# Five places instead of seven in a bidirectional scan, and two more column pairs by seven products

## The chip, the cores and the metric

The kernel runs on one core of a Trainium2 chip. The metric is the device time of one execution in microseconds. The engines are TensorE (PE, matrix products; PEld is its weight load), VectorE (DVE), ScalarE (ACT), GpSimd (POOL) and SyncE (SP, which issues most transfers). Each engine takes its instructions in order; they wait for each other by semaphores.

## The reference, cut to what matters

One encoder layer on 1024 positions of width 1024, in float32:

```
h    = rmsnorm(x)
proj = h @ w_in                       # 8192 columns: glu 1024, q, v, z_f, z_b, og, g_a, g_b 1024 each
a    = pointwise(silu(layernorm(conv31(glu))))
o    = scan(q, 1 - f_f, v, f_f) + flip(scan(flip(q), flip(1 - f_b), flip(v), flip(f_b)))   # 8 heads of 128
       # per head: S_t = diag(f_t) S_{t-1} + k_t v_t^T,  o_t = S_t^T q_t
b    = (rmsnorm per head of o * silu(og)) @ o_w
x    = x + (sigmoid(g_a) * a + sigmoid(g_b) * b) @ w_out
x    = x + (silu(conv3(h2 @ w_gate)) * (h2 @ w_up)) @ w_down,   h2 = rmsnorm(x)
out  = rmsnorm(x)
```

The change touches the projection `h @ w_in`, where and how its columns are computed, and the scan over the heads.

## The kernel before, in words

**Products.** A float32 product is made of three fast ones (`mm3`, L147 to L149): each operand is split into a high and a low part, the split being a copy on ScalarE and a subtraction on VectorE (L123). A *tile* is 128 columns of the projection (`std_job`): 8 steps in depth x 3 x 2 halves of 512 positions = 48 products. A *pair* (`pair_job`) takes two tiles of columns and computes them as a 2 x 2 block product with seven products in place of eight (Strassen and Winograd): 7 x 4 x 3 = 84 products, with sums of weights and of results besides. 56 column tiles are in the list `todo`; the first 2 x `NPAIRS` of them are done in pairs, the others are *filler tiles*.

**Pieces.** Jobs are generators. One `fill(1)` of a `Stream` emits one piece, six products, at that place of the program. PE's order is the order of emission; the other engines' orders are set by a scheduler.

**Stages around the change.** The convolution with 31 taps runs on VectorE (`conv_steps`, L953 and L956: 4 x 31 steps), and after each tap `s_pairs.fill(CONV_FILL)` emits pieces of pairs. Then comes the LayerNorm, with more pieces of pairs, and the pairs are drained. Then comes the scan of the eight heads in two halves of 512 positions each, 16 halves in all, with the filler tiles and the pointwise product's tiles (`dense`) between its steps.

**The scan.** Inside a half, the decays are not applied position by position. Positions are doubled up: at level h (1, 2, 4, ... 64), every block of h positions is scored against its neighbour block, with keys and queries scaled by the decay up to the border between them. Keys `kG` and queries `qF` hold both directions; at each level they are multiplied in place by the block's total decay (`tb`), and `tb` is formed for the next level (`double`, three VectorE steps at L1052). A level of h up to 16 is 16 small products of 32 x 32 (`level`, L1103), whose stationary side is a copy `A` of the keys that interleaves the two directions (`key_blocks`, a ScalarE copy, L1083); the queries are read from `qF` itself. The levels of 32 and 64 are products by block (`blocks`, L1167). The diagonal is 16 x 2 small products (L1138), the two directions adding up in the bank. The results of the small levels are picked out of the bank into `D` through masks (`copy_predicated` on VectorE, L1153, L1187, L1189). A wide product of zeros (`none`, L1182) first fills the bank that levels 32 and 64 write only in part. `scan_states` transposes the doubled keys (L1203, banks `tr`), copies them (`kT`) and forms the states `Sf` and `Sb`; `scan_outputs` forms a head's outputs (L1253), which are squared and scaled on ScalarE (L1258, L1272), transposed back (L1279, banks `tr`) and multiplied by the gate on VectorE (L1281). A head's outputs run beside the next head's scan (`pending`).

**Places.** `scan_base` (levels 1, 2, 4) of the next half and `scan_levels` and `scan_states` (levels 8 to 64, states) of the present half run in step. Each `yield` of the latter two is a *place*: `between` emits `FILL` pieces of filler, one step of the next half's base and one step of the pending outputs. Before, a half has 4 + 3 = 7 places. PSUM has eight banks: three for `mm`, two for `sc`, two for `tr` and one for `ob`.

Of the kernel before, what the change touches and what calls it, by code (L numbers as in the profile page):

```python
# [10 lines left out]
F32 = mybir.dt.float32  # L11
# [5 lines left out]
AX = mybir.AxisListType  # L17

P = 128
FILL = 1.3  # L20
CONV_FILL = 1.6
NPAIRS = 19
LN_FILL = 6
LN_LAST = 12
GLU_FIRST = 4
# [21 lines left out]
def tile_hybrid_encoder(  # L47
# [54 lines left out]
    def page(pool, tag, bufs, dt=F32):  # L102
        return pool.tile([P, H], dt, tag=tag, name=nm(tag), bufs=bufs)
# [941 lines left out]


    hp = tc.alloc_tile_pool(name="heads", bufs=1, reuse_waits="tile")
    none = hp.tile([P, H], mybir.dt.bfloat16, name="none")
    G.memset(none, 0.0)

    def tt(o, a, b, op=ALU.mult):
# [25 lines left out]
    def pairs(t, h, other=H):  # L1077

        return view(t, 0, [[other + h, 2], [2 * h, H // (2 * h)], [1, h]])

    def key_blocks(kG, h):
        A_t = page(hp, "A", 3)
        A.copy(pairs(A_t, h, 0), pairs(kG, h))  # L1083
        return A_t

    def slot(b, n):
        return b[:, n * P : (n + 1) * P]
# [7 lines left out]
    def each():  # L1095
        for c in range(4):
            for g in range(0, P, 32):
                yield c * P + g, slice(g, g + 32), slice(32 * c, 32 * c + 32)

    def level(b, A_t, qF, h):  # L1100

        for at, g, o in each():
            T.matmul(  # L1103
                b[g, o].rearrange("p (b x e) -> p b x e", x=2, e=h),
                A_t[:, at : at + 32],
                view(qF, at, [[2 * h, 16 // h], [H + h, 2], [1, h]]),
                start=True,
                stop=True,
            )

    def double(kG, qF, tb, h, to=None):

        n, nb = H // (2 * h), H // h
        tt(pairs(kG, h), pairs(kG, h), view(tb, 1, [[nb - 1, 2], [2, n], [0, h]]))
        tt(pairs(qF, h), pairs(qF, h), view(tb, nb + 1, [[-(nb + 1), 2], [2, n], [0, h]]))
        if to is None:
            tn = hp.tile([P, 2, n], F32, tag=f"tb{h}", name=nm("tb"), bufs=2)
            to = view(tn, 0, [[n, 2], [1, n]])
        else:
            tn = None  # L1120
        tt(to, view(tb, 0, [[nb, 2], [2, n]]), view(tb, 1, [[nb, 2], [2, n]]))
        return tn

    def scan_base(ins):


        q, f, kG, ks = ins
        qF = hp.tile([P, 2, H], F32, tag="qF", name=nm("qF"), bufs=4)
        D_t = hp.tile([P, 4, 32], F32, tag="D", name=nm("D"), bufs=3)
        for d in range(2):  # L1130
            V.tensor_scalar(kG[:, d, :], kG[:, d, :], ks[:, d : d + 1], None, op0=ALU.mult)
        A_t = key_blocks(kG, 1)
        tt(qF, view(q, 0, [[0, 2], [1, H]]), view(f, H, [[-H, 2], [1, H]]))
        yield
        b = bank("sc")
        for at, g, o in each():
            for d in range(2):
                T.matmul(  # L1138
                    slot(b, 3)[g, o],
                    kG[:, d, at : at + 32],  # L1140
                    q[:, at : at + 32],
                    start=d == 0,
                    stop=d == 1,
                )
        tb = f
        for n, h in enumerate((1, 2, 4)):
            level(slot(b, n), A_t, qF, h)
            tb = double(kG, qF, tb, h)
            A_t = key_blocks(kG, 2 * h)
            yield  # L1150
        A.copy(D_t, near(slot(b, 2)))
        for n, m in ((0, m_1), (1, m_2), (3, m_d)):
            V.copy_predicated(D_t, over(m), near(slot(b, n)))  # L1153
        yield qF, kG, A_t, tb, D_t

    def scan_levels(base, S_t, Tt):


        qF, kG, A_t, tb, D_t = base

        def blocks(b, h):

            for c in range(0, H, P):
                for s0 in range(0, P, h):
                    t0 = s0 ^ h
                    d = s0 // h % 2
                    T.matmul(  # L1167
                        b[s0 : s0 + h, c + t0 : c + t0 + h],
                        kG[:, d, c + s0 : c + s0 + h],
                        qF[:, 1 - d, c + t0 : c + t0 + h],  # L1170
                        start=True,
                        stop=True,
                    )

        for h in (8, 16, 32, 64):
            if h < 32:
                b = bank("ob")
                level(slot(b, 0), A_t, qF, h)
            else:
                if h == 32:  # L1180
                    b = bank("sc")
                    T.matmul(b, none[:, :P], none, start=True, stop=True)  # L1182
                blocks(b, h)
            tb = double(kG, qF, tb, h, view(Tt, 0, [[4, 2], [1, 4]]) if h == 64 else None)
            if h == 8:
                A_t = key_blocks(kG, 16)
                V.copy_predicated(D_t, over(m_8), near(slot(b, 0)))  # L1187
            elif h == 16:
                V.copy_predicated(D_t, over(m_16), near(slot(b, 0)))  # L1189
            elif h == 64:  # L1190
                A.copy(S_t, c4(b))
                for g in range(0, P, 32):
                    A.copy(S_t[g : g + 32, :, g : g + 32], D_t[g : g + 32])
            yield

    def scan_states(i, kG, v, Tt, Sf, Sb):

        half = i % 2
        kTs = []
        for d in range(2):  # L1200
            b = bank("tr")
            for c in range(4):
                T.transpose(b[:, c * P : (c + 1) * P], kG[:, d, c * P : (c + 1) * P], ident)  # L1203
            kT = page(hp, "kT", 2)
            A.copy(kT, b)
            kTs.append(kT)
            yield
        for d in range(2):
            u = bank("sc" if d else "ob")
            for c in range(4):  # L1210
                sl = slice(c * P, (c + 1) * P)
                T.matmul(u[:, sl], kTs[d][:, sl], v[:, c, :], start=True, stop=True)
            u4 = c4(u)
            if d == 0:
                for c in range(4 if half == 0 else 3):
                    nx = Sf[half][:, c + 1, :] if c < 3 else Sf[1][:, 0, :]
                    if half == 0 and c == 0:
                        V.tensor_copy(nx, u4[:, 0, :])
                    else:
                        V.scalar_tensor_tensor(  # L1220
                            nx,
                            Sf[half][:, c, :],
                            Tt[:, half, 0, c : c + 1],
                            u4[:, c, :],
                            op0=ALU.mult,
                            op1=ALU.add,
                        )
            else:

                A.copy(Sb[half][:, 0:3, :], u4[:, 1:4, :])  # L1230
                if half == 1:
                    A.copy(Sb[0][:, 3, :], u4[:, 0, :])
        yield
# [96 lines left out]
    for h in range(NH):  # L1330
        Tt = hp.tile([P, 2, 2, 4], F32, tag="Tt", name=nm("Tt"), bufs=3)
        Sf = [hp.tile([P, 4, DK], F32, tag="st", name=nm("Sf"), bufs=4) for _ in range(2)]
        Sb = [hp.tile([P, 4, DK], F32, tag="st", name=nm("Sb"), bufs=4) for _ in range(2)]
        kept = []
        for half in range(2):
            i = 2 * h + half
            base = cur.result()
            ahead = Base(ins) if i + 1 < NI else None
            ins = scan_inputs(i + 2) if i + 2 < NI else None

            def between(fill):
                dense.fill(fill)
                if ahead is not None:
                    ahead.step(BASE_STEPS)
                pending.fill(1)

            S_t = hp.tile([P, 4, P], F32, tag="S", name=nm("S"), bufs=3)
            vl = load(d_v[h][half])
            for n, _ in enumerate(scan_levels(base, S_t, Tt[:, half])):
                if n == 2:  # L1350
                    b = bank("tr")
                    for c in range(4):
                        T.transpose(b[:, c * P : (c + 1) * P], vl[:, c * P : (c + 1) * P], ident)
                    v = hp.tile([P, 4, DK], F32, tag="v", name=nm("v"), bufs=3)
                    A.copy(v.rearrange("p c e -> p (c e)"), b)
                between(FILL)
            qF, kG = base[:2]
            for _ in scan_states(i, kG, v, Tt, Sf, Sb):
                between(FILL)
            kept.append((S_t, v, qF))  # L1360
            cur = ahead
        pending = Stream(outputs(h, kept, Tt, Sf, Sb))
# [398 lines left out]
```

## Time and profile before

| | |
|---|---|
| median of three runs | 1810.12 us (1809.49 to 1810.22) |
| profiled execution | 1807.26 us, its span 1805.5 us |
| granted TensorE clock | 0.993 of full |
| PE busy over the span | 97% |
| VectorE, ScalarE busy | 67%, 45% |

The span is the time from the first to the last instruction of the profiled execution. Busy time of PE counts a product from its start to its modelled end, and neighbours overlap; the distance between the starts of two products is what one costs.

### The profile page before, as it was taken

How to read it: one execution, taken by the hardware profiler on the slowest of the kernel's cores; microseconds unless marked ns; L12 is line 12 of the kernel's file. 1: busy time of each engine (PE TensorE's matmuls, PEld its weight loads, DVE VectorE, ACT ScalarE, POOL GpSimd, SP SyncE). 2: the span in 40 equal slices, each digit the busy share in tenths (PEclk: the TensorE clock that was granted, in tenths of full speed). 3: DMA queues.
4: the chain of work that ended last, by engine and by line, in shares of the span. 5: the costliest groups of instructions: out<-in, count | busy, mean ns of one | idle time of the engine just before them, and what ended most of it. 6: DMA issues, size and time to landing. Idle time of an engine off the chain costs nothing.

```text
span 1805.5 us, 30702 instructions
## 1 busy us (share of the span) xinstructions
PE 1757.3 (97%) x12150; PEld 1433.9 (79%) x12150; DVE 1213.0 (67%) x1813; ACT 804.1 (45%) x1534; POOL 152.2 (8%) x165
## 2 busy tenths in 40 slices
PE   8989999999999999999989999999999999999997
PEld 6878877888877778877878888878888888888885
DVE  4599999657577777777545666766766766545355
ACT  6344332335466566756552245434434434422123
POOL 1201111000000000000000002011111111000000
PEclk9999999999999999999999999999999999999999
DMA  8658878746652333335358666576776765534233
GB/s 279 215 153 187 190 174 187 203 146 199 209 177 95 120 107 117 118 101 177 112 171 236 200 205 207 142 152 144 147 158 147 151 152 129 161 97 128 82 93 135
DMA packets 321270, 284.48 MB, mean 158 GB/s; under 512 B 14942, under 2 KB 242022, under 8 KB 321126
## 3 DMA queue, kind: packets, MB, share of 16 engines
q1 hardware_dynamic: 279958, 250.01, 44.0%
q0 software_dynamic: 41168, 32.51, 12.8%
q8 instruction: 95, 1.56, 0.3%
q14 instruction: 49, 0.40, 0.1%
HBM read 189.40 MB, written 76.81 MB: 147 GB/s over the span
## 4 chain that ended last, share of the span: by engine, by line
PE 72%; DVE 9%; DMA 7%; ACT 5%; issue 4%; POOL 1%; SPq 1%; POOLq 0%; ACTq 0%; DVEq 0%
PE mm L147 17%; PE mm L149 16%; PE mm L148 16%; PE sc L147 3%; PE sc L149 3%; PE sc L148 3%; DVE acc L956 2%; PE ob L1253 2%; DVE wp L123 2%; PE tr L147 2%; PE tr L149 2%; PE tr L148 2%; DMA ev<-d_ga 1%; PE sc L1103 1%; DMA wr<-in_w_in_dram 1%
## 5 line engine op out<-in xcount | busy, mean ns | idle before, releaser
L147 PE MATMUL mm<-hx,wp 128*128 128x512 f32 x1144 | 463.0, 405 | 9.3 <-DVE ev L718 4.9
L149 PE MATMUL mm<-hx,wp 128*128 128x512 f32 x1144 | 449.9, 393 | 2.1 <-DVE wp L123 2.0
L148 PE MATMUL mm<-hx,wp 128*128 128x512 f32 x1144 | 449.0, 392 | 0.0
L123 ACT CAST wp<-wr 128x1024 fp32r<-128x1024 f32 (+2 forms) x171 | 162.0, 948 | 342.9 <-PE mm L148 258.3
L147 PEld LDWEIGHTS mm<-hx,wp 128*128 128x128 f32 x1144 | 216.6, 189 | 56.1 <-DVE ev L718 7.4
L149 PEld LDWEIGHTS mm<-hx,wp 128*128 128x128 f32 x1144 | 216.3, 189 | 50.6 <-DVE wp L123 3.8
L148 PEld LDWEIGHTS mm<-hx,wp 128*128 128x128 f32 x1144 | 216.7, 189 | 41.3 <-issue 0.2
L123 DVE TENSOR_TENSOR wp<-wr,wp 128x1024 fp32r<-128x1024 f32 (+2 forms) x169 | 186.1, 1102 | 86.0 <-ACT wp L123 85.0
L956 DVE SCALAR_TENSOR_TENSOR acc<-gl,v_b,acc 128x1024 f32<-128x1024 f32 x120 | 149.6, 1284 | 0.4
L1083 ACT COPY A<-kG 128x512 f32<-128x512 f32 x80 | 51.1, 643 | 73.2 <-DVE kG L1052 70.4
L1612 DVE TENSOR_TENSOR xr<-mm,xr 128x512 f32<-128x512 f32 x48 | 33.2, 691 | 73.1 <-PE mm L149 73.1
L367 ACT COPY su<-mm 128x512 f32<-128x512 f32 x82 | 47.5, 579 | 71.6 <-PE mm L149 70.6
L1052 DVE TENSOR_TENSOR kG<-kG,tb 128x512 f32<-128x512 f32 x96 | 66.2, 690 | 18.6 <-PE sc L1167 9.6
L1052 DVE TENSOR_TENSOR qF<-qF,tb 128x512 f32<-128x512 f32 x96 | 66.0, 688 | 13.9 <-PE sc L1103 9.9
L123 ACT CAST wq<-sw 128x1024 fp32r<-128x1024 f32 x41 | 43.1, 1050 | 64.4 <-PE mm L148 25.2
L1461 DVE SCALAR_TENSOR_TENSOR tm<-gp,v_a,tm 128x512 f32<-128x512 f32 x88 | 66.0, 750 | 2.0
L147 PE MATMUL mm<-hy,wp 128*128 128x512 f32 x164 | 64.6, 394 | 1.4 <-ACT su L367 1.4
L147 PE MATMUL sc<-hy,wq 128*128 128x512 f32 x164 | 64.7, 394 | 0.0
L148 PE MATMUL mm<-hy,wp 128*128 128x512 f32 x164 | 64.3, 392 | 0.0
L149 PE MATMUL sc<-hy,wq 128*128 128x512 f32 x164 | 64.2, 391 | 0.0
L147 PE MATMUL tr<-hx,wp 128*128 128x512 f32 x164 | 64.0, 390 | 0.0
L149 PE MATMUL tr<-hx,wp 128*128 128x512 f32 x164 | 63.9, 389 | 0.0
(350 smaller groups left out, 3433.4 us busy)
## 6 DMA issues: line engine op xcount, KB each, us to landing
wr<-in_w_in_dram SPq DMA_DIRECT2D x56, 512.0 KB, 4.6
wr<-in_ffn_w_up_dram SPq DMA_DIRECT2D x24, 512.0 KB, 4.9
sw<-in_ffn_w_up_dram SPq DMA_DIRECT2D x44, 256.0 KB, 3.6
d_g<-ft SPq DMA_DIRECT2D x44, 256.0 KB, 2.4
sw<-in_ffn_w_up_dram POOLq DMA_DIRECT2D x20, 512.0 KB, 8.0
sw<-in_w_in_dram SPq DMA_DIRECT2D x38, 256.0 KB, 3.6
d_z<-ev SPq DMA_DIRECT2D x32, 256.0 KB, 3.6
zi<-d_z SPq DMA_DIRECT2D x32, 256.0 KB, 3.1
```

The source lines that it names most:

```text
L123: parts = A.copy(hi, src), eng.tensor_tensor(lo, src, hi.bitcast(F32), op=ALU.subtract)
L147: T.matmul(acc, whi[:, k, :], ahi, start=first, stop=False, skip_group_check=again)
L148: T.matmul(acc, whi[:, k, :], alo, start=False, stop=False, skip_group_check=again)
L149: T.matmul(acc, wlo[:, k, :], ahi, start=False, stop=last, skip_group_check=again)
L367: A.copy(t, acc)
L956: V.scalar_tensor_tensor(acc, g[:, k : k + S], tap(k), acc, op0=ALU.mult, op1=ALU.add)
L1052: V.tensor_tensor(o, a, b, op=op)
L1083: A.copy(pairs(A_t, h, 0), pairs(kG, h))
L1103: T.matmul(b[g, o].rearrange("p (b x e) -> p b x e", x=2, e=h), A_t[:, at : at + 32], view(qF, at, [[2 * h, 16 // h], [H + h, 2], [1, h]]) ...
L1253: T.matmul(o[:, sl], l, r, start=(n == 0), stop=(n == len(terms) - 1))
L1461: V.scalar_tensor_tensor(c, g[:, o + k : o + k + H], vec("fdw", k * NF + j), c, op0=ALU.mult, op1=ALU.add,)
L1612: V.tensor_tensor(xr[i][half], acc, xr[i][half], op=ALU.add)
```

## The change

- `NPAIRS` goes from 19 to 21: four more column tiles are made in pairs, and 14 filler tiles are left of 18. `CONV_FILL` goes from 1.6 to 1.85 pieces after each tap.
- The scan has five places in a half: levels 1, 2, 4 and the diagonal are scored in one place, levels 8 and 16 in another, and both keys are transposed in one place. `FILL` goes from 1.3 to 1.41 pieces.
- To score several levels at once, each level's queries are copied too (`woven`, on ScalarE, for levels 2, 4 and 8; level 1's are written by VectorE at once in that form). `A` has eight buffers in place of three.
- The two directions' keys are added on VectorE (`k_d`), so the diagonal is 16 products in place of 32.
- The zeros are 16 products of 32 x 32 in place of one of 128 x 512.
- `double` is cut into `double_keys`, `double_queries` and `totals`.

```diff
-FILL = 1.3
-CONV_FILL = 1.6
-NPAIRS = 19
+FILL = 1.41
+CONV_FILL = 1.85
+NPAIRS = 21
...
-    none = hp.tile([P, H], mybir.dt.bfloat16, name="none")
+    none = hp.tile([P, 32], mybir.dt.bfloat16, name="none")
...
-    def key_blocks(kG, h):
-        A_t = page(hp, "A", 3)
-        A.copy(pairs(A_t, h, 0), pairs(kG, h))
-        return A_t
+    def woven(t, h):
+
+        t_h = page(hp, "A", 8)
+        A.copy(pairs(t_h, h, 0), pairs(t, h))
+        return t_h
...
-    def level(b, A_t, qF, h):
-
+    def level(b, A_t, Q_t):
         for at, g, o in each():
-            T.matmul(
-                b[g, o].rearrange("p (b x e) -> p b x e", x=2, e=h),
-                A_t[:, at : at + 32],
-                view(qF, at, [[2 * h, 16 // h], [H + h, 2], [1, h]]),
-                start=True,
-                stop=True,
-            )
+            T.matmul(b[g, o], A_t[:, at : at + 32], Q_t(at), start=True, stop=True)
...
-        A_t = key_blocks(kG, 1)
-        tt(qF, view(q, 0, [[0, 2], [1, H]]), view(f, H, [[-H, 2], [1, H]]))
+        k_d, Q1 = page(hp, "A", 8), page(hp, "A", 8)
+        tt(k_d, kG[:, 0, :], kG[:, 1, :], ALU.add)
+        A1 = woven(kG, 1)
...
+        double_keys(kG, f, 1)
+        double_queries(qF, pairs(Q1, 1, 0), f, 1)
+        tb = totals(f, 1)
+        yield
+        A2, Q2 = woven(kG, 2), woven(qF, 2)
+        double_keys(kG, tb, 2)
+        double_queries(qF, pairs(qF, 2), tb, 2)
+        tb = totals(tb, 2)
+        A4, Q4 = woven(kG, 4), woven(qF, 4)
         yield
         b = bank("sc")
-        for at, g, o in each():
-            for d in range(2):
-                T.matmul(
...
+        for n, (k_t, q_t) in enumerate(((k_d, q), (A1, Q1), (A2, Q2), (A4, Q4))):
+            level(slot(b, n), k_t, row(q_t))
+        double_keys(kG, tb, 4)
+        double_queries(qF, pairs(qF, 4), tb, 4)
+        tb = totals(tb, 4)
+        A8, Q8 = woven(kG, 8), woven(qF, 8)
+        yield
...
-        for h in (8, 16, 32, 64):
...
+        b = bank("ob")
+        level(slot(b, 0), A8, row(Q8))
+        level(slot(b, 1), A16, lambda at: view(qF, at, [[H + 16, 2], [1, 16]]))
+        tb = double(tb, 16)
+        for n, m in enumerate((m_8, m_16)):
+            V.copy_predicated(D_t, over(m), near(slot(b, n)))
+        yield
+        b = bank("sc")
+        for at, g, _ in each():
+            T.matmul(b[g, at : at + 32], none, none, start=True, stop=True)
+        blocks(b, 32)
+        tb = double(tb, 32)
+        yield
+        blocks(b, 64)
+        double(tb, 64, view(Tt, 0, [[4, 2], [1, 4]]))
...
@@ scan_states
             kTs.append(kT)
-            yield
+        yield
```

More of the change, by code (lines that the diff above doesn't have):

```diff
@@ L1098, in each, with row, double_keys, double_queries @@
                 yield c * P + g, slice(g, g + 32), slice(32 * c, 32 * c + 32)
-    def level(b, A_t, qF, h):
+    def level(b, A_t, Q_t):
         for at, g, o in each():
-            T.matmul(
-                b[g, o].rearrange("p (b x e) -> p b x e", x=2, e=h),
-                A_t[:, at : at + 32],
-                view(qF, at, [[2 * h, 16 // h], [H + h, 2], [1, h]]),
-                start=True,
-                stop=True,
-            )
-    def double(kG, qF, tb, h, to=None):
+            T.matmul(b[g, o], A_t[:, at : at + 32], Q_t(at), start=True, stop=True)
+    def row(t):
+        return lambda at: t[:, at : at + 32]
+    def double_keys(kG, tb, h):
         n, nb = H // (2 * h), H // h
         tt(pairs(kG, h), pairs(kG, h), view(tb, 1, [[nb - 1, 2], [2, n], [0, h]]))
-        tt(pairs(qF, h), pairs(qF, h), view(tb, nb + 1, [[-(nb + 1), 2], [2, n], [0, h]]))
+    def double_queries(qF, q, tb, h):
+        n, nb = H // (2 * h), H // h
+        tt(pairs(qF, h), q, view(tb, nb + 1, [[-(nb + 1), 2], [2, n], [0, h]]))
+    def totals(tb, h, to=None):
+        n, nb = H // (2 * h), H // h
+        tn = None
         if to is None:
-            tn = hp.tile([P, 2, n], F32, tag=f"tb{h}", name=nm("tb"), bufs=2)
+            tn = hp.tile([P, 2, n], F32, tag=f"tb{h}", name=nm("tb"), bufs=1 if h < 8 else 2)
             to = view(tn, 0, [[n, 2], [1, n]])
-        else:
-            tn = None
         tt(to, view(tb, 0, [[nb, 2], [2, n]]), view(tb, 1, [[nb, 2], [2, n]]))
@@ L1131, in scan_base @@
             V.tensor_scalar(kG[:, d, :], kG[:, d, :], ks[:, d : d + 1], None, op0=ALU.mult)
-        A_t = key_blocks(kG, 1)
-        tt(qF, view(q, 0, [[0, 2], [1, H]]), view(f, H, [[-H, 2], [1, H]]))
+        k_d, Q1 = page(hp, "A", 8), page(hp, "A", 8)
+        tt(k_d, kG[:, 0, :], kG[:, 1, :], ALU.add)
+        A1 = woven(kG, 1)
+        odd = H // 2
+        tt(
+            pairs(Q1, 1, 0),
+            view(q, 0, [[1, 2], [2, odd], [1, 1]]),
+            view(f, H, [[1 - H, 2], [2, odd], [1, 1]]),
+        )
@@ L1134, in scan_base @@
+        tt(
+            view(qF, 1, [[H - 1, 2], [2, odd]]),
+            view(q, 1, [[-1, 2], [2, odd]]),
+            view(f, H + 1, [[-(H + 1), 2], [2, odd]]),
+        )
+        double_keys(kG, f, 1)
[7 more added lines that the diff above has]
+        A4, Q4 = woven(kG, 4), woven(qF, 4)
         yield
@@ L1135, in scan_base @@
         b = bank("sc")
-        for at, g, o in each():
-            for d in range(2):
[L1138 to L1149, printed above, removed]
-            yield
@@ L1151, in scan_base @@
-        A.copy(D_t, near(slot(b, 2)))
-        for n, m in ((0, m_1), (1, m_2), (3, m_d)):
-            V.copy_predicated(D_t, over(m), near(slot(b, n)))
-        yield qF, kG, A_t, tb, D_t
+        for n, (k_t, q_t) in enumerate(((k_d, q), (A1, Q1), (A2, Q2), (A4, Q4))):
[5 more added lines that the diff above has]
+        yield
+        A.copy(D_t, near(slot(b, 3)))
@@ L1156, in scan_levels @@
+        for n, m in enumerate((m_d, m_1, m_2)):
+            V.copy_predicated(D_t, over(m), near(slot(b, n)))
+        double_keys(kG, tb, 8)
+        double_queries(qF, pairs(qF, 8), tb, 8)
+        tb = totals(tb, 8)
+        A16 = woven(kG, 16)
+        yield
+        yield qF, kG, tb, D_t, A8, Q8, A16
     def scan_levels(base, S_t, Tt):
-        qF, kG, A_t, tb, D_t = base
+        qF, kG, tb, D_t, A8, Q8, A16 = base
         def blocks(b, h):
@@ L1173, in blocks, with double @@
                     )
-        for h in (8, 16, 32, 64):
[L1176 to L1194, printed above, removed]
+        def double(tb, h, to=None):
+            double_keys(kG, tb, h)
+            double_queries(qF, pairs(qF, h), tb, h)
+            return totals(tb, h, to)
+        b = bank("ob")
[13 more added lines that the diff above has]
+        double(tb, 64, view(Tt, 0, [[4, 2], [1, 4]]))
+        A.copy(S_t, c4(b))
+        for g in range(0, P, 32):
+            A.copy(S_t[g : g + 32, :, g : g + 32], D_t[g : g + 32])
+        yield
     def scan_states(i, kG, v, Tt, Sf, Sb):
@@ L1206, in scan_states @@
             kTs.append(kT)
-            yield
+        yield
         for d in range(2):
@@ L1349, in tile_hybrid_encoder @@
             for n, _ in enumerate(scan_levels(base, S_t, Tt[:, half])):
-                if n == 2:
+                if n == 1:
                     b = bank("tr")
```

## The prediction

> **What bounds the kernel now.** I read the page's busy time first, then the busy time by stretch, then the order of time on TensorE (PE) inside one stage. The page:
>
> ```profile
> span 1805.5 us, 30702 instructions
> PE 1757.3 (97%) x12150; PEld 1433.9 (79%) x12150; DVE 1213.0 (67%) x1813; ACT 804.1 (45%) x1534; POOL 152.2 (8%) x165
> ```
>
> PE is busy nearly everywhere, so the first question for any edit is how much PE time it adds or removes, and the second whether PE still gets its operands in time. A mean over the span hides the second, so the stretches come next (microseconds, then PE, PEld, VectorE, ScalarE and GpSimd busy with their instruction counts).
>
> ```profile
> 85.00:337.00 252.00, 242.44 (x1050) 197.08 (x1049) 241.43 (x259) 97.50 (x137) 37.52 (x38) 0.99 0.77 179
> 337.00:470.00 133.00, 132.37 (x584) 108.06 (x583) 80.12 (x107) 53.76 (x84) 3.31 (x4) 1.00 0.59 185
> 508.00:896.00 388.00, 376.89 (x5970) 304.35 (x5963) 286.25 (x597) 242.02 (x568) 12.83 (x14) 0.99 0.37 118
> 701.40:721.84 20.44, 20.44 (x361) 16.15 (x363) 17.67 (x42) 12.72 (x26) 0.00 (x0) 1.00 0.38 118
> 701.40:749.67 48.27, 47.37 (x768) 38.30 (x772) 36.22 (x76) 32.64 (x77) 1.83 (x2) 1.00 0.35 113
> 749.67:799.78 50.11, 47.82 (x766) 38.55 (x770) 39.06 (x82) 31.16 (x75) 1.83 (x2) 0.99 0.36 114
> ```
>
> The first row is the convolution's taps beside the first pairs: VectorE is full (241 of 252 us) and PE loses 9.6 us. The second is pairs beside the LayerNorm: PE is full, 133.0 / 584 = 0.228 us for a product of 512 columns. The third is the scan with its filler: PE idles 388.0 - 376.9 = 11.1 us, about 1.4 us for each of the eight heads. The last two rows are one head each (mean 49.2 us, VectorE 37.6, ScalarE 31.9). The fourth is the first half of a head, where PE never waits although VectorE is at 86%: a VectorE this full is bearable while its work comes in the right order. So the scan is bound by PE, with VectorE next behind it.
>
> **The change, part by part.** *Pairs and filler.* Two more pairs are 2 x 7 x 4 x 3 = 168 products, 168 x 0.228 = +38.3 us in the second stretch's conditions, where VectorE has 53 us in 133 free for their splits. Four filler tiles fewer are 4 x 2 x 8 x 3 = 192 products, -43.7 us. By 5 x 1.41 = 7.05 pieces in a half in place of 7 x 1.3 = 9.1 all of this leaves the scan stage: 33 pieces of six products, 5.6 us per head. About ten pieces stay for its end, as before.
>
> *Taps spread wider.* I take nothing for this. In the order of instructions on VectorE, which a scheduler sets, the taps stand against the pairs' own VectorE work exactly alike in both kernels (10 taps before the pairs' first result, 31 before the seventh, 123 before the 33rd); only PE's list was stretched. What hides it is that VectorE itself sets the pace of that stretch.
>
> *Products on the diagonal, zeros, and places.* The order of time on PE (start, length, operation):
>
> ```profile
> 656.95 0.39 PE L148 MATMUL mm<-hx,wp 128*128 128x512 f32 x1
> 657.17 0.40 PE L149 MATMUL mm<-hx,wp 128*128 128x512 f32 x1
> 657.50 0.47 PE L1103 MATMUL sc<-qF,A 128*32 128x32 f32 x32
> 657.89 0.69 PE L1167 MATMUL sc<-qF,kG 128*64 128x64 f32 x16
> 658.51 0.50 PE L147 MATMUL mm<-hx,wp 128*128 128x512 f32 x1
> 658.85 0.39 PE L148 MATMUL mm<-hx,wp 128*128 128x512 f32 x1
> ...
> 701.33 0.76 PE L1138 MATMUL sc<-q,kG 128*32 128x32 f32 x58
> 701.99 0.54 PE L1103 MATMUL sc<-qF,A 128*32 128x32 f32 x28
> 702.46 0.39 PE L1182 MATMUL sc<-none 128*128 128x512 bf16 x1
> 702.78 0.46 PE L1167 MATMUL sc<-qF,kG 128*32 128x32 f32 x32
> 703.17 0.65 PE L1353 MATMUL tr<-ident,tm 128*128 128x128 f32 x4
> 703.58 0.48 PE L147 MATMUL mm<-hx,wp 128*128 128x512 f32 x1
> ```
>
> Lengths overlap; the distance between starts is the price. A level of 16 small products takes 657.50 to 657.89 = 0.39 us. From 701.33 to 702.46 stand the 32 products on the diagonal (both directions) and one level: 1.13 - 0.39 = 0.74 us for the 32. Adding the two keys first halves them: 16 x 0.37 = -5.9 us.
>
> The zeros are one wide product now, 702.46 to 702.78 = 0.32 us. They become 16 small bf16 products, each with a weight load of its own in the program. The trace has none of these. Bounds: 0.20 us (half of a level: the trace records each of a level's fp32 products twice, x32, and the bf16 one once) and 0.78 us (each of the 32 written instructions at 0.39 / 16). I take 0.52, nearer to the level's 0.39 because the shape is the same: +0.2 in each half, +3.2 us, between -1.9 and +7.4. The Trainium skill, "TensorE: Matmul & The Clock Gate", section "Back-to-back issue gap", has small matmuls never start closer than about 25 ns; by that estimate alone the zeros would take 0.40 us, the edit +1.3, and the sum would be 1.9 us lower. The trace's 0.39 / 16 = 24 ns agrees for fp32; no run here yet shows it for these.
>
> Going from filler to small work and back costs too: the first small product starts 657.50 - 657.17 = 0.33 us after the last filler product, and the second filler product 658.85 - 658.51 = 0.34 us after the first, where 0.23 is usual: 0.21 us for a round trip. Seven places become five, so two fewer in each half: 32 x 0.21 = -6.7 us.
>
> Work alone: 38.3 - 43.7 - 5.9 + 3.2 - 6.7 = **-14.8 us**.
>
> *What VectorE and ScalarE get.* From VectorE's order of time, and the page's groups of the copies and of the weight splits (busy us, mean ns, idle before and whom it ended with):
>
> ```profile
> 725.92 1.22 DVE L1052 TENSOR_TENSOR qF<-q,f 128x1024 f32<-128x1024 f32 x1
> 727.06 0.69 DVE L1052 TENSOR_TENSOR kG<-kG,tb 128x512 f32<-128x512 f32 x1
> 727.66 0.69 DVE L1052 TENSOR_TENSOR qF<-qF,tb 128x512 f32<-128x512 f32 x1
> 748.56 0.75 DVE L1281 SCALAR_TENSOR_TENSOR ev<-tr,v_a,og 128x512 f32<-128x512 f32 x1
> 749.22 0.69 DVE L1052 TENSOR_TENSOR qF<-qF,tb 128x512 f32<-128x512 f32 x1
> ```
>
> ```profile
> L1083 ACT COPY A<-kG 128x512 f32<-128x512 f32 x80 | 51.1, 643 | 73.2 <-DVE kG L1052 70.4 <-PE sc L1103 2.4
> L123 ACT CAST wp<-wr 128x1024 fp32r<-128x1024 f32 (+2 forms) x171 | 162.0, 948 | 342.9 <-PE mm L148 258.3
> L123 DVE TENSOR_TENSOR wp<-wr,wp 128x1024 fp32r<-128x1024 f32 (+2 forms) x169 | 186.1, 1102 | 86.0 <-ACT wp L123 85.0
> ```
>
> VectorE starts a 512-wide step every 0.60 us. Per head it gains two key sums (1.2) and 2 x 0.06 for the first query product cut in two (2 x 0.60 against 1.14), and loses half a filler weight's split (-0.55): 38.4 us. ScalarE gains six query copies, 6 x 0.64 = 3.9, and loses half a cast (-0.5): 35.3. PE needs per head 49.2 less 5.6, 0.74 and 0.84, plus 0.4: 42.4 us. VectorE then stands at 90%, ScalarE at 83%. This is nothing by itself (in the fourth row 86% cost PE nothing), but less slack covers each wait.
>
> *Where PE waits anew.* The transposes share two banks ("tr"). In the changed order on PE, in the second half of a head, the transposes of an earlier head's second output are followed at once by those of the two keys, with no filler between; the last of the three needs the bank of the first, which VectorE's multiplication at L1281 (0.75 us) must have read. PE is there 0.41 us later (four transposes, 703.17 to 703.58). At best the wait is 0.75 - 0.41 = 0.3 us. In most heads that multiplication stands on VectorE behind a query doubling (0.69), and this one behind its copy on ScalarE (0.64): 2.08 - 0.41 = 1.7 us. I take 1.0, the middle, eight times: **+8.0 us**. Behind it queue the states, the next filler and the next levels; nothing regains it. The other waits I traced are covered: the doublings before L1186's blocks have 12 filler products (2.7 us) and the level's four copies a whole place, 42.4 / 10 = 4.2 us.
>
> Sum: -14.8 + 8.0 = **-6.8 us**. The profiled execution took 1807.3 us (1.8 around its span) and would take 1800.5; it lies 2.9 under the median of the runs, 1810.1, which would become **1803.3**. A measurement of this kernel tells about 0.2% (3.6 us) from no change.
>
> **The rivals.** *Slower: the two engines behind PE set the scan's pace.* VectorE takes its list in order. Level copies double in number (a key and a query copy each), so it stands at a doubling until ScalarE has made both. In a head's second half ScalarE also squares and scales the outputs of the head before. If the doublings by 32, which PE's 64-wide blocks need, queue behind the next half's first pair of copies (2 x 0.64) and doublings (2 x 0.60), PE waits another 2.5 us per head on top of the 1.0: 8 x 3.5 - 14.8 = +13, 1823 us. It decides from 14.8 / 8 = 1.85 us of new waiting per head. For it: 70.4 us of ScalarE's idle time before these copies already end on VectorE's keys, so the two wait on each other in turns; in the last heads' order the doublings stand just so. Against it: in the earlier heads' order the doublings by 32 come first. The Trainium skill, "TensorEngine Tiling (Array Packing)", section "PSUM Bottleneck", says that packing small products speeds up TensorE but not the emptying of its banks, which may become the bottleneck. That is an argument for this side; the trace agrees only weakly so far:
>
> ```profile
> PE ob L1103 <- DVE D L1187: 4.9, 7, 2.0
> PE ob L1103 <- DVE Sf L1220: 2.1, 5, 0.9
> ```
>
> (waits of PE in the scan: us in all, times, longest).
>
> *Faster: no new waits.* Levels 8 and 16 now share one filling of "ob", so the first of these rows goes: -14.8 - 4.9 = -19.7, 1790.4 us, if the "tr" wait is also hidden. Against it: 0.3 us per head seems sure.
>
> *The taps do move.* If PE got back the 9.6 us that it loses in the first stretch, -6.8 - 9.6 = -16.4, 1793.7 us. The unchanged order speaks against it.
>
> **How the numbers follow.** The forecast, a small gain of 3.6 to 12 us, has 0.36; the two faster rivals 0.10 and 0.03; the slower one (over +3.6) 0.34; waits that just eat the gain, 0.17. So faster 0.49, same 0.17, slower 0.34. The range reaches from near the faster rivals, 1792, to the slower rival's price, 1824; for the forecast alone, zeros from -5.1 to +4.2 against what I took and the wait from 0.3 to 1.7 us, it is 1793 to 1813.
>
> **What would show it.** Right: the scan's stage shorter by some 46 us and the pairs' longer by 38; a head near 43.4 us; the wait before the second key transposes at 0.3 to 1.7 us; the diagonal at 16 products; the taps ending near 337 us still. Wrong: a head above 44.3 us (no gain left), PE waiting for a doubled key or query at the 64-wide blocks, zeros above 0.8 us, the pairs' stretch at over 0.23 us a product, or a first stretch that is longer or shorter than 252 us.

## The result, and the profile after

The changed kernel took 1798.83 us (median of five runs, 1797.39 to 1800.54) against 1810.12 (1804.75 to 1811.04): a ratio of 0.9945, 95% interval 0.9929 to 0.9961. The forecast was 1803.3, a small gain, and the time lies inside the range. The profiled execution took 1798.56 us. That the sum came out near is luck: two large errors of opposite sign cancel in it, as the experiments show. One run further down, of the kernel with the taps close again, took 4006 us at a granted clock of 0.434 and is left out of its median. First the page of after:

```profile
span 1796.8 us, 30229 instructions
PE 1736.1 (97%) x11854; PEld 1426.9 (79%) x11854; DVE 1225.8 (68%) x1861; ACT 832.8 (46%) x1589; POOL 151.0 (8%) x165
```

PE's busy time fell by 21.2 us, the span by only 8.7. So 12.5 us of the saved work came back as idle time. The stretches (the columns as in the prediction; two heads of the scan are the last two rows):

```profile
84.00:336.00 252.00, 241.42 (x1047) 196.32 (x1046) 241.12 (x259) 96.56 (x136) 37.52 (x38) 0.99 0.76 178
336.00:510.00 174.00, 170.29 (x748) 139.74 (x747) 94.72 (x120) 63.96 (x95) 2.44 (x4) 0.99 0.55 173
...
662.12:705.84 43.72, 40.89 (x711) 34.49 (x714) 36.28 (x81) 33.71 (x81) 1.84 (x2) 0.96 0.38 116
705.84:747.62 41.78, 39.31 (x711) 33.03 (x714) 36.16 (x81) 33.95 (x82) 1.83 (x2) 1.00 0.36 116
```

The stretch of the taps is as it was. In the stretch of the pairs PE now loses 3.7 us by 510, and a product takes 174 / 748 = 0.233 us with its waits, over the 0.23 that the prediction named as a sign of being wrong; in the row shown of before PE lost 0.6. A head takes 41.8 us at full clock and 43.7 at 0.96, against 49.2 before. The list of PE's waits over the whole span says where the idle time is (us in all, times, longest):

```profile
PE mm L147 <- DVE ev L718: 13.8, 7, 4.5
PE tr L1226 <- DVE ev L1304: 9.1, 5, 2.8
PE tr L1226 <- ACT kT L1228: 4.6, 2, 2.5
...
PE sc L1186 <- DVE qF L1052: 2.3, 4, 1.2
```

The first row was 4.9 us before; rows two and three are new; the wait of "ob" for `D` (4.9 us before) is gone.

**The new wait at the key transposes.** PE and VectorE side by side (start, length, in brackets the idle time before):

```profile
726.01 0.46 PE L1103 MATMUL sc<-q,A 128*32 128x32 f32 x32
726.29 1.05 PE L1103 MATMUL sc<-A,A 128*32 128x32 f32 x96
727.04 0.68 DVE L1052 TENSOR_TENSOR kG<-kG,tb 128x512 f32<-128x512 f32 x1
727.27 0.65 PE L1302 MATMUL tr<-ident,tm 128*128 128x128 f32 x4
727.64 0.68 DVE L1052 TENSOR_TENSOR qF<-qF,tb 128x512 f32<-128x512 f32 x1
727.76 0.60 PE L1226 MATMUL tr<-ident,kG 128*128 128x128 f32 x4
728.25 0.68 DVE L1052 TENSOR_TENSOR tb<-f 128x512 f32<-128x512 f32 x1
728.85 0.68 DVE L1052 TENSOR_TENSOR kG<-kG,tb 128x512 f32<-128x512 f32 x1
729.45 0.74 DVE L1304 SCALAR_TENSOR_TENSOR ev<-tr,v_a,og 128x512 f32<-128x512 f32 x1
730.25 0.66 PE L1226 MATMUL tr<-ident,kG 128*128 128x128 f32 x4 [1.89 <-DVE ev L1304]
```

The second key's transposes (730.25) need the bank that the output's transposes (727.27) filled. The multiplication that reads it, L1304 (L1281 before), ran at 729.45 only: after the transposes begin, VectorE starts three more steps of the doublings, 0.60 us each (727.64 to 728.85), and then the multiplication.

**The new wait in the pairs.** PE's order of time, with VectorE's last steps before the wait ends:

```profile
515.64 0.39 PE L149 MATMUL sc<-hx,wq 128*128 128x512 f32 x1
516.42 1.30 DVE L994 TENSOR_TENSOR cx<-cx,tm 128x512 f32<-128x512 f32 x2
...
518.83 1.01 DVE L995 TENSOR_SCALAR cx<-cx,v_a 128x512 f32<-128x512 f32 x2
519.74 0.69 DVE L718 TENSOR_TENSOR ev<-su,mm 128x512 f32<-128x512 f32 x1
520.49 0.53 PE L147 MATMUL mm<-hx,wp 128*128 128x512 f32 x1 [4.46 <-DVE ev L718]
520.83 0.61 PE L148 MATMUL mm<-hx,wp 128*128 128x512 f32 x1
521.24 0.63 PE L149 MATMUL mm<-hx,wp 128*128 128x512 f32 x1
...
523.80 0.60 PE L149 MATMUL mm<-hx,wp 128*128 128x512 f32 x1
524.23 0.41 PE L147 MATMUL mm<-hx,wp 128*128 128x512 f32 x1
```

PE stands 4.46 us for a sum of the pair (L718) that VectorE, busy with the LayerNorm (L994, L995), makes late. Then the granted clock is 0.50 from 520.83 to 524.24: from 520.49 to 524.23 nine products take 3.74 us, 0.42 each, in place of 9 x 0.228 = 2.05. The wait's full price is 4.46 + 1.7 = 6.2 us. The Trainium skill, "TensorE: Matmul & The Clock Gate", section "HAM oscillation", has the clock fall to half after gaps over about 3.4 us. This wait agrees; a shorter one at the end of this document does not.

### The profile page after: what moved, and what is told of

Same layout as the page of the kernel before. It is cut to its first block, busy times and chain, and to the rows that moved or that the text cites. A ratio compares the mean times of both kernels' runs of the same rounds, so it can differ in the third digit from the quotient of the medians.

```text
span 1796.8 us, 30229 instructions
## 1 busy us (share of the span) xinstructions
PE 1736.1 (97%) x11854; PEld 1426.9 (79%) x11854; DVE 1225.8 (68%) x1861; ACT 832.8 (46%) x1589; POOL 151.0 (8%) x165
## 4 chain that ended last, share of the span: by engine, by line
PE 72%; DVE 9%; DMA 7%; issue 5%; ACT 4%; POOL 1%; SPq 0%; POOLq 0%; ACTq 0%; DVEq 0%
PE mm L147 17%; PE mm L148 17%; PE mm L149 17%; PE sc L147 3%; PE sc L149 3%; PE sc L148 3%; DVE acc L956 3%; PE ob L1276 2%; DMA sw<-in_w_in_dram 2%; DMA wr<-wr 2%; PE tr L147 2%; PE tr L148 2%; PE tr L149 2%; DVE wp L123 1%; DMA wr<-sw 1%
## 5 line engine op out<-in xcount | busy, mean ns | idle before, releaser
L147 PE MATMUL mm<-hx,wp 128*128 128x512 f32 x1096 | 442.5, 404 | 18.2 <-DVE ev L718 13.8
L149 PE MATMUL mm<-hx,wp 128*128 128x512 f32 x1096 | 431.9, 394 | 1.9 <-DVE wp L123 1.9
L148 PE MATMUL mm<-hx,wp 128*128 128x512 f32 x1096 | 431.5, 394 | 0.0
L147 PEld LDWEIGHTS mm<-hx,wp 128*128 128x128 f32 x1096 | 208.3, 190 | 64.6 <-DVE ev L718 16.8
L149 PEld LDWEIGHTS mm<-hx,wp 128*128 128x128 f32 x1096 | 208.2, 190 | 48.2 <-DVE wp L123 3.2
L148 PEld LDWEIGHTS mm<-hx,wp 128*128 128x128 f32 x1096 | 208.6, 190 | 40.7 <-issue 0.5
L147 PE MATMUL mm<-hy,wp 128*128 128x512 f32 x172 | 67.5, 393 | 1.4 <-ACT su L367 1.4
L148 PE MATMUL mm<-hy,wp 128*128 128x512 f32 x172 | 67.4, 392 | 0.0
L147 PE MATMUL sc<-hy,wq 128*128 128x512 f32 x172 | 67.4, 392 | 0.0
L149 PE MATMUL sc<-hy,wq 128*128 128x512 f32 x172 | 67.3, 391 | 0.0
L147 PE MATMUL tr<-hx,wp 128*128 128x512 f32 x172 | 67.2, 390 | 0.0
L149 PE MATMUL tr<-hx,wp 128*128 128x512 f32 x172 | 67.0, 389 | 0.0
L148 PE MATMUL tr<-hx,wp 128*128 128x512 f32 x172 | 67.0, 389 | 0.0
```

Source lines behind the costliest of these rows:

```text
L147: T.matmul(acc, whi[:, k, :], ahi, start=first, stop=False, skip_group_check=again)
L148: T.matmul(acc, whi[:, k, :], alo, start=False, stop=False, skip_group_check=again)
L149: T.matmul(acc, wlo[:, k, :], ahi, start=False, stop=last, skip_group_check=again)
```

## The experiments

The theory after the result: the regrouping by itself gains more than the whole change (10 to 14 us by the forecast for its run); the wait at the key transposes, and a LayerNorm that falls on the wrong part of a pair because of the taps' count, give back part of it. Times are medians; ratios are to the kernel before on the same chip, with 95% intervals.

**The two halves of the change apart.** *Pairs alone*, on the old scan:

```diff
-FILL = 1.3
-CONV_FILL = 1.6
-NPAIRS = 19
+FILL = 1.01
+CONV_FILL = 1.85
+NPAIRS = 21
```

> The kernel before with 21 pairs, 1.85 pieces after each tap and 1.01 pieces of filler at each of its seven places (about ten pieces stay for the end, as always). My theory: work -5.5 us, the LayerNorm's wait of 8 us that the changed kernel shows comes with the pairs, and the scan's old order, with a doubling of queries that must wait for PE to have read them, waits more as the filler shrinks: 1808 to 1818 us, no gain. Rival (the gain is the two pairs' spared products): 1804 or less.

Measured: 1816.87 us, 1.0041 (1.0026 to 1.0055), a loss of 7.4 us, inside the range expected. *The regrouped places alone*, on after:

```diff
-FILL = 1.41
-CONV_FILL = 1.85
-NPAIRS = 21
+FILL = 1.82
+CONV_FILL = 1.6
+NPAIRS = 19
```

> The changed kernel with 19 pairs, 1.6 pieces after each tap and 1.82 pieces of filler at each of its five places: the scan's regrouping alone. My theory: diagonal -5.9, zeros -3.4, round trips -6.7, levels scored together about -5, new waits at the key transposes +9 or less since more filler covers them, no LayerNorm wait: 1796 to 1800 us. Rival (the gain is the spared products, the regrouping only makes room): 1807 to 1811.

Measured: 1786.02 us, 0.9877 (0.9858 to 0.9896), a gain of 22 us, and 10 us below the range expected: the work shrank about as that forecast had it, but the waits as a whole hardly grew, where 9 us were allowed for. So the places bring everything, and the pairs take 12 us of it (0.9945 - 0.9877 = 0.0068). This run also shows where the regrouping's gain lies, since it has as much filler as before. Five heads of the kernel before, then five of this one, between the same points of the order:

```profile
625.75:871.99 246.24, 239.04 (x3823) 193.57 (x3825) 183.03 (x380) 157.02 (x376) 9.15 (x10) 0.99 0.38 123
```

```profile
604.24:838.62 234.38, 226.35 (x3648) 189.94 (x3647) 184.35 (x408) 173.22 (x409) 9.44 (x10) 0.99 0.41 131
```

A head is (246.24 - 234.38) / 5 = 2.4 us shorter, with the same 547 filler products in each stretch. Adding up the distances between starts, 10.1 of these 11.9 us are in the small products, 2.8 in the filler and its edges, and waits grew by 1.0. PE's groups of the levels over the whole span, of the kernel before and then of this one (busy us, mean ns | idle):

```profile
L1103 PE MATMUL sc<-qF,A 128*32 128x32 f32 x1536 | 25.1, 204 | 2.9 <-issue 2.7
L1103 PE MATMUL ob<-qF,A 128*32 128x32 f32 x1024 | 14.7, 198 | 7.3 <-DVE D L1187 4.9 <-DVE Sf L1220 2.1
L1138 PE MATMUL sc<-q,kG 128*32 128x32 f32 x1024 | 14.0, 202 | 0.0
```

```profile
L1103 PE MATMUL sc<-A,A 128*32 128x32 f32 x1536 | 17.3, 199 | 0.9 <-ACT A L1084 0.9
L1103 PE MATMUL ob<-qF,A 128*32 128x32 f32 x512 | 7.8, 199 | 0.0
L1103 PE MATMUL ob<-A,A 128*32 128x32 f32 x512 | 7.3, 199 | 0.0
L1103 PE MATMUL sc<-q,A 128*32 128x32 f32 x512 | 7.3, 199 | 0.0
```

The diagonal went from 14.0 to 7.3 us (`sc<-q,A`), and the 80 other levels, the same products, from 39.8 to 32.4: 0.50 us of busy time for a level that stands alone, 0.40 for one in company.

**The taps' count.** *Taps close again*, the new scan and 21 pairs kept:

```diff
-CONV_FILL = 1.85
+CONV_FILL = 1.6
```

> The changed kernel with 1.6 pieces after each tap as before; the 31 pieces go behind the LayerNorm. My theory: taps end at 335 to 337 us as in both kernels, so the spreading itself gives nothing; but the LayerNorm falls on other products of the pairs, and its two waits of 8.2 us at the banks of the pairs (VectorE's normalisation stands ahead of the pairs' results) shrink or move: 1791 to 1801 us. Rival (the spreading gives PE room in the taps' stretch): 1804 or more, with more than 10.6 us of PE idle in 84 to 336.

Measured: 1787.61 us, 0.9888 (0.9868 to 0.9908), by the ratios 10 us better than after and below the range expected. The scan begins 11.6 us earlier (its first diagonal product at 548.8 us, in after at 560.4). PE's waits in its stretch of pairs (336 to 548 us), where after has 8.2 us in two waits:

```profile
PE mm L147 <- DVE ev L718: 0.7, 1, 0.7
```

That left two readings: filler spread wide is dear as such, or only where in a pair the LayerNorm falls counts. 124 taps at 1.6, 1.83 and 1.85 pieces end 2.4, 2.9 and 5.4 pieces into a pair of 14. So 1.83 tells them apart:

```diff
-CONV_FILL = 1.85
+CONV_FILL = 1.83
```

> The changed kernel with 1.83 in place of 1.85 pieces after each tap: the LayerNorm's two halves stand three pieces earlier on PE, on the same products of a pair (the spread of the mean square after five and six pieces of it, as with 1.6), but as late in the stage as in the changed kernel. My theory (what costs 10 us is on which product of the pair the LayerNorm falls, since VectorE normalises ahead of a result whose bank PE needs next): as with 1.6, 1788 to 1792 us, and the waits of 8.2 us after the taps are gone. Rival (the spreading itself, the LayerNorm's nearness to the end of the pairs): 1797 to 1800.

Measured: 1789.25 us, 0.9886 (0.9868 to 0.9903), as with 1.6; 2.0 us of waits for L718 are left in the stretch of pairs. Spread is harmless; the place in the pair decides. Pairs alone, above, had the same two waits (8.2 us), with its old scan.

**The order at the transposes.** *Outputs first*: the pending outputs' step stands ahead of the base's in `between`, which puts the scores between the two groups of transposes.

```diff
+                pending.fill(1)
                 if ahead is not None:
                     ahead.step(BASE_STEPS)
-                pending.fill(1)
```

> The changed kernel with the pending outputs' step emitted ahead of the next half's base step at each place, so that the second output's transposes stand before the 64 small products (1.26 us) instead of right before the key transposes. My theory: the 9.1 us that PE waits at the key transposes for VectorE's gate multiplication come from the two shared banks; with 1.26 us more between them five such waits lose some 6 us, and the kernel takes about 1793 us. Rival (VectorE's list sets the pace, whatever PE's order): the wait turns up at the next doubling or block and the time stays at 1799.

Measured: 1798.15 us, 0.9945 (0.9926 to 0.9965): no change. PE's waits in the scan:

```profile
PE ob L1103 <- DVE Sf L1243: 10.7, 8, 2.3
PE sc L1186 <- DVE qF L1052: 4.6, 7, 1.6
PE tr L1226 <- DVE ev L1304: 0.4, 1, 0.4
```

The named wait went from 9.1 to 0.4 us, and others took its place, as the rival had it, though mostly at levels 8 and 16, which now wait for "ob", which `Sf` is still read from. The run is not one of PE's order alone: the scheduler set VectorE's list anew, and in six heads the multiplication now starts 0.6 to 1.4 us after the second output's transposes begin, in after 1.5 to 3.6.

*Another bank* for the second key's transposes, with the taps at 1.6 and three counts of pairs (`FILL` 1.41, 1.61 and 1.82 for 21, 20 and 19):

```diff
-            b = bank("tr")
+            b = bank("sc" if d else "tr")
```

> The changed kernel with 1.6 pieces after each tap, and the second key transposes of a half written to a bank of the two named sc in place of the two named tr. They then wait for nothing that VectorE's gate multiplication reads. My theory (the 13.7 us of waits at the key transposes are the price of two banks): they fall below 4 us, and since VectorE's list is the next to set the pace only part is won: 1781 to 1786 us, against 1789 with 1.6 alone. Rival (the wait just moves, as in the run with the outputs first): 1787 to 1791.

> The same bank with 20 pairs, 1.6 pieces after each tap and 1.61 pieces of filler. Its waits at the key transposes were 8.8 us. My theory: 1781 to 1785 us. Rival (the wait moves): 1787.

> The same bank with 19 pairs, 1.6 pieces after each tap and 1.82 pieces of filler, the regrouping alone. Its waits at the key transposes were 6.7 us. My theory: 1780 to 1784 us. Rival (the wait moves): 1786.

Measured: 21 pairs 1778.5 us (1775.93 to 1780.71), 0.9818 (0.9793 to 0.9843); 20 pairs 1778.7, 0.9822 (0.9797 to 0.9846); 19 pairs 1780.0, 0.9831 (0.9806 to 0.9856). Two of the three are below the range expected, and the rival (the wait just moves) is out. With 21 pairs that is 9 us by the medians, 13 by the ratios, better than without the bank (the runs are from two chips, on which the kernel before took 1808.5 and 1813.23 us), and the best of all, 33 us under the kernel before by the ratio (0.0182 x 1810). PE's waits in the scan (548 to 862 us) with 21 pairs:

```profile
PE ob L1103 <- DVE Sf L1243: 3.5, 3, 1.9
PE sc L1186 <- DVE qF L1052: 3.4, 6, 1.2
PE ob L1235 <- ACT kT L1228: 1.7, 3, 0.9
PE ob L1276 <- DVE Sb L1328: 0.9, 1, 0.9
```

No wait at the key transposes is left, where there were 13.7 us; about half of that comes back in the others (9.5 us in all here, 15.8 in the scan of after). From the first half's diagonal to the last half's the scan takes 305.6 us here and 313.1 with the taps at 1.6 alone. The new order only moved the wait; a free bank took about half of it away. The Trainium skill, "Perfetto Trace Analysis", section "Optimizing Tensor Performance", lets independent groups rotate through different banks so that emptying one overlaps the next; these runs agree, and put 9 to 13 us to it.

**How many pairs.** *20 pairs*, without the bank (`FILL` 1.61, `CONV_FILL` 1.6):

```diff
-FILL = 1.41
-CONV_FILL = 1.85
-NPAIRS = 21
+FILL = 1.61
+CONV_FILL = 1.6
+NPAIRS = 20
```

> The changed kernel with 20 pairs, 1.6 pieces after each tap and 1.61 pieces of filler at each place: between the kernels with 19 and with 21 pairs, at the same places of the LayerNorm. My theory (two pairs spare 5.5 us, but the scan's waits rise as its filler shrinks, 11 to 16 us from 19 to 21): flat, 1785 to 1789 us. Rival (the spared products come through): 1783 or less; or a step in the waits: 1790 or more.

Measured: 1789.06 us, 0.9874 (0.9853 to 0.9895). With the taps at 1.6, 19, 20 and 21 pairs make 0.9877, 0.9874 and 0.9888; with the bank 0.9831, 0.9822 and 0.9818. No count differs from its neighbours by more than the intervals.

**Is small work on the path?** *The diagonal twice* (16 products more in each half, on top of taps at 1.6):

```diff
-            level(slot(b, n), k_t, row(q_t))
+            for _ in range(2 if n == 0 else 1):
+                level(slot(b, n), k_t, row(q_t))
```

> The changed kernel with 1.6 pieces after each tap, and the diagonal's 16 products emitted twice (the same result written twice): 256 small products more. My theory (PE's work in the scan is on the path that sets the end): at 0.28 to 0.39 us for 16, +4.5 to +6.2 us over the kernel with 1.6 alone, so 1793 to 1795 us. Rival (VectorE and ScalarE set the scan's pace by now): +2 us or less, 1789 to 1791.

Measured: 1797.14 us, 0.9918 (0.9899 to 0.9936): 0.0030 above the kernel without it, 5.4 us, or 0.34 us for each of 16 levels. That is more than expected, the intervals of the two overlap at their edges, and this run's profile also has 4 us more of waiting for L718 ahead of the scan, so the time alone cannot tell the theory from its rival. The traces can: from the first half's diagonal to the last half's the scan takes 320.8 us against 313.1. Of these 7.7 us 4.3 lie between the starts of small products, 0.29 us for each of 15 levels more, and 0.7 in waits; the rest is filler, with two more stretches at a granted clock of 0.50. The waits did not shrink to make room, so small products are on the path at about their price in the order of time.

**Why are levels together cheaper?** One idea was that copied queries, read in a row, stream faster. *Queries in strides* for level 8, whose scores this kernel therefore changes:

```diff
-        level(slot(b, 0), A8, row(Q8))
+        level(slot(b, 0), A8, lambda at: view(qF, at, [[16, 2], [H + 8, 2], [1, 8]]))
```

> The changed kernel with level 8 reading its queries from the two directions' pages in runs of eight (as the kernel before did) in place of the copy's 32 in a row; the copy is still made. The queries it reads are one scaling too far, so the scores of this level differ. It asks whether small products are cheaper since their queries lie in a row: the changed kernel's level 8 takes 0.28 us from its first product to level 16's first (736.75 to 737.03), where the kernel before has 0.39 us for a level. If reading in a row is what is cheaper: 0.33 us or more for level 8. If it is that levels stand one after the other: 0.28 again.

Measured: 1797.56 us in a single run. Levels 8 and 16 stand from 737.40 to 738.09 there, 0.69 us, and from 736.75 to 737.45 in after, 0.70 us, and it is alike in all 16 halves. Runs of eight are not what was dear. Shorter runs were not tried here, but in the kernel before the lone levels of 2 to 16, read in runs of 2 to 16, all take 0.39 us. What is left is that levels stand together.

## Why the prediction was right, and where it was not

**Diagonal (-5.9): right.** The group's busy time shrank by 14.0 - 7.3 = 6.7 us.

**Zeros (+3.2): wrong in sign.** The place of the zeros and of levels 8 and 16 in after:

```profile
736.44 0.39 PE L149 MATMUL mm<-hx,wp 128*128 128x512 f32 x1
736.75 0.46 PE L1103 MATMUL ob<-A,A 128*32 128x32 f32 x32
737.03 0.49 PE L1103 MATMUL ob<-qF,A 128*32 128x32 f32 x32
737.45 0.50 PE L147 MATMUL mm<-hx,wp 128*128 128x512 f32 x1
...
738.70 0.40 PE L149 MATMUL mm<-hx,wp 128*128 128x512 f32 x1
739.03 0.28 PE L1208 MATMUL sc<-none 128*32 128x32 bf16 x16
739.14 0.47 PE L1186 MATMUL sc<-qF,kG 128*32 128x32 f32 x32
```

From 739.03 to 739.14 the zeros cost 0.11 us, against 0.32 before: 16 x -0.21 = -3.4, below the lower bound of -1.9. The step that failed is that the price was taken near an fp32 level's. By the Trainium skill's 25 ns they would have cost 0.40; this row gives 0.11 / 16 = 7 ns from start to start. The single records behind it begin in sets of four, a set every 25 ns (739.070, 739.095, 739.120), so the figure fits a set here and not a product. The 0.39 / 16 = 24 ns that the prediction took for agreement had the way to the next group in it: level 8 takes 0.28 / 16 = 17 ns. In 12 of the 16 halves the zeros cost the same 0.11 us; in the other four the blocks start 0.19 to 0.86 us after them, twice behind a wait for the doubled queries.

**Round trips (-6.7): too large, and the saving beside them was left out.** In the five heads above PE goes from filler to small work and back 70 times before and 50 times after; filler and edges shrank by 2.8 us, which is 8 / 5 x 2.8 = 4.5 us for the kernel. The step that failed is that each level got 0.39 us wherever it stands: that levels in company are cheaper was put at nothing. In the rows of after the diagonal and three levels take 726.01 to 727.27 = 1.26 us, and levels 8 and 16 take 0.28 and 0.42, the second with the way back in it. In the traces of the five heads the diagonal and the five levels of a half took 1.13 + 4 x 0.39 = 2.69 us before and 1.28 + 0.69 = 1.97 with the places alone (medians), 11.5 us less in 16 halves; the diagonal has about 6 of them, the company of the levels about 5. (The 39.8 - 32.4 = 7.4 us above are busy time, in which a lone level's end overlaps what follows.) The regrouping's work was forecast at -5.9 + 3.2 - 6.7 = -9.4 us; the five heads give 8 / 5 x (10.1 + 2.8) = 21 us. Some 2 of the 21 are in none of these terms, and where they lie stays open.

**Pairs and filler (38.3 - 43.7 = -5.4): wrong, +12.** The taps were as forecast: the last ends at 336.6 us in both kernels. What was missed is that the count of pieces after each tap shifts the pairs against the LayerNorm behind them. The text priced all 168 products at the unhindered 0.228 us. Two waits of 8.2 us with slow products after each, some 11.6 us in all, are the difference between `CONV_FILL` 1.85 and 1.6 (10 us by the ratios). The pairs alone then come to -5.4 + 11.6 = +6.2, and measured +7.4. In the new scan even well-placed pairs bring nothing (0.9888 against 0.9877): less filler, more waiting at the transposes (13.7 us with 21 pairs, 6.7 with 19).

**The wait at the key transposes (+8.0): right in place and main cause, near in sum by luck.** It is 9.1 us in five waits of up to 2.8, not eight of 1.0. ScalarE's copies `kT` add 4.6 in two more heads at the same transposes, which the text did not price: 13.7 us in all. The longest was over the bound of 1.7, since in the four longest three to five VectorE steps start between the transposes and the multiplication, not one.

**A head near 43.4 us: right as a number.** Six heads from 618.9 to 875.2 us have a mean of 42.7, but the terms behind the 43.4 are those above. From the first half's diagonal to the last half's the scan took 364.4 us before and 314.7 after, 50 less where some 46 were forecast. It begins 53 us later (507.5 and 560.4), where 38 were forecast: the LayerNorm's waits are in it, and with 19 pairs too the first scores come 8 us later (515.5).

**The rivals.** *Slower*: half of its mechanism is there, PE waiting at L1186 for doubled queries, but 2.3 us in four waits, far from 2.5 a head. Three of them are at the 64-wide blocks, which the prediction named as a sign of being wrong and took for covered. *No new waits*: the "ob" wait for `D` did go, as it said; the other half of its condition, no wait at "tr", held only with another bank. *Taps move*: no.

So the small gain was forecast from -9.4, -5.4 and +8.0; it came from about -21 of work in the scan and the -5.4, and in return +13.7 of waits at the transposes and some +11 of LayerNorm; of the old waits in the scan some 8 went (10.6 us before, 2.5 after besides the transposes).

## What to carry to other kernels

Forecast a change in two parts as two runs: the sum was right here by luck, and each half far off. When a piece count changes, ask which later work on another engine the shifted pieces will meet; 0.02 pieces a tap were worth 10 us. When a wait is for a bank, give the group another bank before trying another order; the one order tried here only moved the wait.

## What was not expected of the hardware

Sixteen small bf16 products with a weight load each took 0.11 us, fp32 ones of the same shape 0.28 (736.75 to 737.03).

A wait on PE can cost more than its length: 1.4 times for the 4.46 us. A shorter one can too. PE's order of time in after, at another second key's transposes:

```profile
686.87 0.66 PE L1226 MATMUL tr<-ident,kG 128*128 128x128 f32 x4 [2.77 <-DVE ev L1304]
...
688.46 0.63 PE L148 MATMUL mm<-hx,wp 128*128 128x512 f32 x1
688.88 0.63 PE L149 MATMUL mm<-hx,wp 128*128 128x512 f32 x1
689.31 1.91 PE L1235 MATMUL ob<-v,kT 128*128 128x128 f32 x8
691.01 1.30 PE L1235 MATMUL sc<-v,kT 128*128 128x128 f32 x8
692.06 0.48 PE L147 MATMUL mm<-hx,wp 128*128 128x512 f32 x1
```

A wait of 2.77 us, and the products behind it are slow from 688.46 on: 0.42 us to the next start, and 1.70 us for the first eight state products, where the next eight take 1.05. After the wait of 1.89 us shown above nothing of the kind is in the trace. The length alone does not decide: after a wait of 2.05 us the granted clock is 0.50 from 643.72 to 647.13, and after one of 2.50 us it is 1.00 from 771.94 to 775.40. What decides stays open. The head with the longer wait is the one of clock 0.96 and 43.7 us above, the head with the shorter one that of 1.00 and 41.8.
